# Feed-forward and conv outputs made one tile at a time, from all inner tiles

## The chip, the cores and the metric

The kernel runs on one core of one Trainium2 chip. A time is device microseconds (us) of one execution, the median of several. A core has five engines that run side by side, each in its own order: TensorE (PE in the profile: matrix products, with its weight loads shown apart as PEld), VectorE (DVE), ScalarE (ACT), GpSimd (POOL), and SyncE (SP), which starts most DMAs. On-chip memory is SBUF; PE writes into PSUM, eight banks of 128 x 512 floats here.

## The reference, cut to what matters

A trunk of two layers over 256 tokens of 1024 features, in full fp32. Each layer has a feed-forward, a mixer (attention with pooling in layer 0, a short convolution in layer 1), and another feed-forward; each of these six sub-layers takes a normed input that a vector c shifts and scales, and is added to the stream through a gate that c drives too.

```
mod = (silu(c) @ w_ada[l] + b_ada[l])                       # 9 vectors of 1024 per layer: shift, scale, gate x 3
h = rmsnorm(x, norm_g[l, j]) * (1 + scale) + shift
x = x + 0.5 * gate * ((silu(h @ wg) * (h @ wu)) @ wd)       # feed-forward: 1024 -> 2816 -> 1024
x = x + gate * mixer(h)                                     # attention and pooling, or conv
```

## The kernel before, in words

**Layout.** Features lie on partitions, tokens along the free dimension: a feature tile is 128 x 256. The stream x is eight such tiles, `xt`. A feed-forward has 22 inner tiles (2816 = 22 x 128).

**Products.** A product of 128 x 128 weights with a tile is made of three matmuls of 256 columns: high weights by high activations, low weights by high, high by low (`mm`, L312). "High" is a value rounded to fp32r, "low" what is left. Weights arrive by DMA into `raw` (four slots of 2 MB) and are split on the chip: ACT casts the high part `wh` (L357), then DVE or, every fourth time, POOL subtracts to give the low part `wl` (L373). Five buffers hold split weights, some 8 to 12 us ahead of their use.

**Steps.** The program is a list of steps in the order of PE's work, most of them 24 matmuls: a step has its products, what evacuates them (`post`), and work that is put off by one or two steps. The order on every engine is this program order; each engine runs its own list strictly in that order.

**Feed-forward.** The inner tiles come in six chunks of 3 or 4: gate products, up products, then the chunk's down products, which are added for all eight output tiles in four PSUM banks. The last chunk's down steps (12 matmuls per output tile) finish the output tiles one after the other: DVE adds gate times result to the stream in SBUF (L660), `take` lets ACT make the square and the high part of the next sub-layer's input, and two steps later DVE adds the square to the sum of squares (L498) and makes the low part (L499).

**Norm put off.** The next sub-layer doesn't wait for its norm. Its first seven products (six in attention, eight in conv; `raw_steps`) take x * g * (1 + scale), called `xh` and `xl`, with 258 columns. When the sum of squares is complete, PE sums it over the partitions (`total`, L506), DVE works out 1 / rms, PE spreads it (L523), and DVE copies it to `rtile` (L527). Then POOL (`nx` L531, `nh` L541), ACT (`ah` L542) and DVE (`al` L546) make the eight normed tiles that all later products take. In a feed-forward the seven products are those of the first chunk (3 gates, 3 ups) and one gate of the second; the first chunk's down products come next, and they take only the first chunk's activations.

**Modulation in the background.** The vectors that c drives need 128 more multiply-adds of 128 x 1024 rows on DVE ("macs", `ada_mac`, L160 and L162). Each takes one 512 KB transfer (`adaw`, four buffers). Eight or sixteen macs make one accumulator `acc`; PE then transposes it (L189) and DVE reduces it (L193). `RATES` says how many macs are handed out per step; `flush` hands out at once, in one row, all that the next sub-layer still needs, and the transposes behind them. `flush` is called on entering the last chunk's up steps and down steps, the conv's first output step, and a step of attention.

## Time and profile before

| | |
|---|---|
| time, median of 3 runs | 1089.36 us (1088.84 to 1092.68) |
| span of the profiled execution | 1092.0 us |
| PE busy | 1014.1 us, 93% of the span |
| DVE busy | 824.7 us, 76% |
| ACT busy, POOL busy | 503.7 us, 462.5 us |
| DMA, share of 16 engines | 61.6% |

The profile is of one execution. A busy time is the sum over an engine's instructions; since matmuls overlap, PE's pace is better read from the starts of two matmuls. PE runs at one of two granted clocks, 1.2 or 2.4 GHz; the profile gives the mean as a share of the full one (0.957 over the whole span).

### The profile page before, as it was taken

How to read it: one execution, taken by the hardware profiler on the slowest of the kernel's cores; microseconds unless marked ns; L12 is line 12 of the kernel's file. 1: busy time of each engine (PE TensorE's matmuls, PEld its weight loads, DVE VectorE, ACT ScalarE, POOL GpSimd, SP SyncE). 2: the span in 40 equal slices, each digit the busy share in tenths (PEclk: the TensorE clock that was granted, in tenths of full speed). 3: DMA queues.
4: the chain of work that ended last, by engine and by line, in shares of the span. 5: the costliest groups of instructions: out<-in, count | busy, mean ns of one | idle time of the engine just before them, and what ended most of it. 6: DMA issues, size and time to landing. Idle time of an engine off the chain costs nothing.

```text
span 1092.0 us, 19601 instructions
## 1 busy us (share of the span) xinstructions
PE 1014.1 (93%) x7894; PEld 986.1 (90%) x7894; DVE 824.7 (76%) x1118; ACT 503.7 (46%) x905; POOL 462.5 (42%) x346
## 2 busy tenths in 40 slices
PE   3799999998698799999998999999899989999998
PEld 2799999988567799999997999999889988999998
DVE  3857876888988889799888978896778788534442
ACT  3344544445445554345454544345554455444453
POOL 6712322265943672232166522234664567112223
PEclk9789999998879899999998999999999989999999
DMA  9588998773173429988865497996344534735601
GB/s 349 206 307 297 335 359 311 261 264 125 59 270 111 159 94 361 355 304 319 298 243 188 189 351 265 352 359 231 107 152 155 173 117 147 275 122 209 232 1 40
DMA packets 98634, 247.15 MB, mean 226 GB/s; under 512 B 4768, under 2 KB 22228, under 8 KB 98544
## 3 DMA queue, kind: packets, MB, share of 16 engines
q1 hardware_dynamic: 98288, 245.78, 61.6%
q8 instruction: 62, 1.02, 0.4%
q14 instruction: 28, 0.23, 0.1%
q0 software_dynamic: 256, 0.12, 0.0%
HBM read 244.84 MB, written 1.05 MB: 225 GB/s over the span
## 4 chain that ended last, share of the span: by engine, by line
PE 69%; DVE 17%; issue 6%; POOL 5%; ACT 2%; DMA 0%; SPq 0%; DVEq 0%; ACTq 0%; POOLq 0%
PE pu L312 41%; PE acc L312 25%; DVE acc L162 5%; DVE ssum L498 3%; POOL nh L541 2%; POOL nx L531 2%; DVE wl L373 2%; ACT wh L357 1%; DVE xt L660 1%; DVE xl L499 1%; POOL ssum L1407 1%; DVE al L322 1%; PE pu L1310 1%; PE pu L1015 1%; DVE rs_t L439 0%
## 5 line engine op out<-in xcount | busy, mean ns | idle before, releaser
L373 POOL TENSOR_TENSOR wl<-raw,wh 128x1024 fp32r<-128x1024 f32 (+1 forms) x162 | 328.3, 2038 | 528.8 <-ACT wh L357 443.0
L357 ACT CAST wh<-raw 128x1024 fp32r<-128x1024 f32 (+2 forms) x408 | 345.1, 860 | 136.7 <-PE acc L312 86.8
L312 PE MATMUL pu<-ah,wh 128*128 128x256 f32 x1304 | 371.4, 285 | 0.4 <-ACT ah L542 0.4
L312 PE MATMUL pu<-al,wh 128*128 128x256 f32 x1304 | 370.3, 284 | 0.5 <-DVE al L546 0.5
L312 PE MATMUL pu<-ah,wl 128*128 128x256 f32 x1304 | 370.2, 284 | 0.0
L373 DVE TENSOR_TENSOR wl<-raw,wh 128x1024 fp32r<-128x1024 f32 (+2 forms) x246 | 271.1, 1110 | 74.5 <-ACT wh L357 74.4
L312 PE MATMUL acc<-ah,wh 128*128 128x256 f32 x896 | 259.3, 289 | 10.3 <-ACT ah L319 6.5
L312 PE MATMUL acc<-al,wh 128*128 128x256 f32 x896 | 257.8, 288 | 3.2 <-DVE al L322 3.2
L312 PE MATMUL acc<-ah,wl 128*128 128x256 f32 x896 | 256.8, 287 | 0.0
L312 PEld LDWEIGHTS pu<-al,wh 128*128 128x128 f32 x1304 | 251.3, 193 | 0.9 <-DVE al L546 0.9
L312 PEld LDWEIGHTS pu<-ah,wh 128*128 128x128 f32 x1304 | 251.4, 193 | 0.7 <-ACT ah L542 0.7
L312 PEld LDWEIGHTS pu<-ah,wl 128*128 128x128 f32 x1304 | 251.4, 193 | 0.2 <-POOL wl L373 0.2
L162 DVE SCALAR_TENSOR_TENSOR acc<-adaw,cact,acc 128x1024 f32<-128x1024 f32 x119 | 197.1, 1656 | 0.4
L312 PEld LDWEIGHTS acc<-ah,wh 128*128 128x128 f32 x896 | 176.0, 196 | 11.3 <-ACT ah L319 7.3
L312 PEld LDWEIGHTS acc<-al,wh 128*128 128x128 f32 x896 | 175.4, 196 | 4.4 <-DVE al L322 4.3
L312 PEld LDWEIGHTS acc<-ah,wl 128*128 128x128 f32 x896 | 175.7, 196 | 0.0
L319 ACT CAST ah<-sg 128x256 fp32r<-128x256 f32 x88 | 35.6, 407 | 172.1 <-DVE sg L705 157.2
L705 DVE TENSOR_TENSOR sg<-pu,sg 128x256 f32<-128x256 f32 x75 | 31.5, 420 | 79.8 <-PE pu L312 79.6
L312 PE MATMUL pu<-xl,wh 128*128 128x258 f32 x200 | 65.2, 326 | 23.1 <-DVE xl L499 22.3
L697 ACT ACTIVATE sg<-pu 128x256 f32<-128x256 f32 x72 | 27.4, 383 | 111.1 <-PE pu L312 111.1
L312 PEld LDWEIGHTS pu<-xl,wh 128*128 128x128 f32 x200 | 43.3, 216 | 28.6 <-DVE xl L499 28.6
L531 POOL TENSOR_TENSOR nx<-xt,rtile 128x256 f32<-128x256 f32 x48 | 47.3, 990 | 43.0 <-DVE rtile L527 40.9
(187 smaller groups left out, 1117.7 us busy)
## 6 DMA issues: line engine op xcount, KB each, us to landing
adaw<-in_w_ada_dram SPq DMA_DIRECT2D x128, 512.0 KB, 5.7
raw<-in_ffn_wd_dram SPq DMA_DIRECT2D x16, 2048.0 KB, 9.2
raw<-in_ffn_wu_dram SPq DMA_DIRECT2D x15, 2048.0 KB, 10.6
raw<-in_ffn_wg_dram SPq DMA_DIRECT2D x14, 2048.0 KB, 10.3
raw<-in_ffn_wg_dram SPq DMA_DIRECT2D x8, 1536.0 KB, 7.1
raw<-in_ffn_wu_dram SPq DMA_DIRECT2D x8, 1536.0 KB, 7.2
raw<-in_ffn_wd_dram SPq DMA_DIRECT2D x8, 1536.0 KB, 7.3
raw<-in_w_in_c_dram SPq DMA_DIRECT2D x6, 2048.0 KB, 7.8
```

The costliest lines, as they stand in the source:

```text
L162: nc.vector.scalar_tensor_tensor(out=acc, in0=w, scalar=scales[:, k:k + 1], in1=acc, op0=ALU.mult, op1=ALU.add)
L312: nc.tensor.matmul(ps, lhsT=a[:, k, :], rhs=m, start=start and i == 0, stop=stop and i == n - 1, skip_group_check=True)
L319: nc.scalar.copy(hi, src)
L322: nc.vector.tensor_tensor(out=lo, in0=src, in1=hi.bitcast(F32), op=ALU.subtract)
L357: nc.scalar.copy(shaped(hi, r), r)
L373: eng.tensor_tensor(out=shaped(lo, r), in0=r, in1=shaped(hi, r).bitcast(F32), op=ALU.subtract)
L498: nc.vector.tensor_tensor(out=self.s, in0=self.s, in1=q, op=ALU.add)
L499: nc.vector.scalar_tensor_tensor(out=lo[:, 0:T], in0=xt[d], scalar=g, in1=hi[:, 0:T].bitcast(F32), op0=ALU.mult, op1=ALU.subtract)
L531: nc.gpsimd.tensor_tensor(out=a, in0=xt[t], in1=rtile[:, 0:T], op=ALU.mult)
L541: (eng or nc.gpsimd).tensor_scalar(out=h, in0=a, scalar1=g, scalar2=s, op0=ALU.mult, op1=ALU.add)
L697: nc.scalar.activation(out=s, in_=v, func=AF.Silu)
L705: nc.vector.tensor_tensor(out=s, in0=v, in1=s, op=ALU.mult)
```

## The change

- Down products (and the conv's output products) are made one output tile at a time, from all inner tiles: for each of the eight tiles d three steps of 8, 8 and 6 inner tiles (`DOWN`; one step of 8 in conv). All gate and up products come before them, in the order gate, gate, up, up. The chunks are gone, and with them their own buffers for the last chunk's weights.
- High and low activations stand side by side in one tile, so a down product is two matmuls instead of three (`mm2`): high weights by both, 512 columns, and low weights by the high one, 256 columns. The two halves of the PSUM bank are added when the tile is finished.
- `finish` updates the stream inside PSUM: DVE u = b * gate + xt, DVE a = a * gate + u in PSUM; ACT takes the high part, the copy to `xt` and the square from PSUM, DVE the low part and the sum of squares with one operand in PSUM. Low part one step later, sum two steps later; for the last tile both at once.
- Up products stay in PSUM: they are multiplied by the gate there, and split from there.
- Of the deferred products, the first step now takes seven pieces of the input, the second four, then the first step's eighth; `total` stands behind that, ahead of the rest of the second step.
- Weights are fetched in eight slots of 1 MB (256 columns of gate, up and down weights) instead of four of 2 MB.
- `RATES` of the feed-forwards is 0.6, 0.7 and 0.7 macs per step instead of 1.3, 1.3 and 1.4; it counts the down steps in full, where each was counted 0.6 (the last chunk's not at all). `flush` is entered at the third down step of tile 0.
- The result's transposes are put off by one step instead of two, and its last transfers are cut at tiles 6 and 7.

The diff, cut to its core:

```
-FIRST = (4, 4, 3, 3, 4, 4)
-CHUNKS = (3, 3, 4, 4, 4, 4)
-SLOT = 4096
+NF = DFF // P
+OWN = 14
+DOWN = (8, 8, 6)
+SLOT = 2048
...
-ADAB, RAWB = 4, 4
+ADAB, RAWB = 4, 8
...
-RATES = ((-3, 1.3), (4, 1.9), (0, 1.3), (0, 1.4), (1, 1.1), (1, 1.0))
+RATES = ((-3, 0.6), (4, 1.9), (0, 0.7), (0, 0.7), (1, 1.1), (1, 1.0))
...
+    def mm2(bank_, w, xs, start, stop, ks):
+        wh, wl = w
+        both = bank_.rearrange("p (a t) -> p a t", a=2)
+        for i, k in enumerate(ks):
+            x = xs[k]
+            nc.tensor.matmul(both, lhsT=wh[:, i, :], rhs=x, start=start and i == 0, stop=False, skip_group_check=True)
+            nc.tensor.matmul(bank_[:, 0:T], lhsT=wl[:, i, :], rhs=x[:, 0, :], start=False, stop=stop and i == len(ks) - 1,
+                             skip_group_check=True)
...
-        def take(self, d):
+        def take(self, d, a, b):
             g = self.gsc[:, d:d + 1]
             hi, lo = self.xs[d]
-            q = self.square(d)
-            nc.scalar.activation(out=hi[:, 0:T], in_=xt[d], func=AF.Copy, scale=g)
+            nc.scalar.activation(out=hi[:, 0:T], in_=a, func=AF.Copy, scale=g)

             def rest():
-                if q is not None:
-                    nc.vector.tensor_tensor(out=self.s, in0=self.s, in1=q, op=ALU.add)
-                nc.vector.scalar_tensor_tensor(out=lo[:, 0:T], in0=xt[d], scalar=g,
+                nc.vector.scalar_tensor_tensor(out=lo[:, 0:T], in0=a, scalar=g,
                                                in1=hi[:, 0:T].bitcast(F32), op0=ALU.mult, op1=ALU.subtract)
-            return rest
+                nc.scalar.copy(xt[d], a)
...
+                nc.scalar.activation(out=a if b is None else b, in_=a, func=AF.Square)
+
+            def total():
+                if d:
+                    nc.vector.tensor_tensor(out=self.s, in0=a if b is None else b, in1=self.s, op=ALU.add)
+            return rest, total
...
                     if i == 0:
                         st["w0"] = w
-                        mm(st[0], w, self.xs, True, False, range(6))
+                        mm(st[0], w, self.xs, True, False, range(KT - 1))
                     elif i == 1:
-                        mm(st[1], w, self.xs, True, False, range(6))
-                        mm(st[0], st["w0"], self.xs, False, True, range(6, KT))
-                        mm(st[1], w, self.xs, False, True, range(6, KT))
+                        mm(st[1], w, self.xs, True, False, range(4))
+                        mm(st[0], st["w0"], self.xs, False, True, range(KT - 1, KT))
                         self.total()
+                        mm(st[1], w, self.xs, False, True, range(4, KT))
...
+    def finish(d, a, b, gate, target):
+        g = gate[:, d:d + 1]
+        r = xt[d]
+        if b is not None:
+            u = scr.tile([P, T], F32, name=nm("u"), tag="nh")
+            nc.vector.scalar_tensor_tensor(out=u, in0=b, scalar=g, in1=r, op0=ALU.mult, op1=ALU.add)
+            r = u
+        nc.vector.scalar_tensor_tensor(out=a if isinstance(target, Norm) else xt[d], in0=a, scalar=g, in1=r,
+                                       op0=ALU.mult, op1=ALU.add)
+        if not isinstance(target, Norm):
+            return target.take(d)
+        rest, total = target.take(d, a, b)
+        if d < KT - 1:
+            return [(1, rest), (2, total)]
+        rest()
+        total()
+        return []
...
+    def major_steps(acts, piece, parts, gate, target, width=0, ticks=1.0):
+        box = {}
+        k0 = len(steps)
+        starts = [sum(parts[:i]) for i in range(len(parts))]
+        for d in range(KT):
+            for i, (f0, n) in enumerate(zip(starts, parts)):
+                final = i == len(parts) - 1
...
+                    mm2(box[d], w, xs, i == 0, final and m == n, range(f0, f0 + m))
...
+                add(Step(pe, raw=piece(d, i), post=post, ticks=ticks, cost=3 * n,
+                         keep=int(final and d + 1 < width)))
+        def enter():
+            flush()
+            get_ready(target, [0])
+        steps[k0 + len(parts) - 1].enter = enter
...
-                nc.vector.tensor_tensor(out=s, in0=v, in1=s, op=ALU.mult)
+                nc.vector.tensor_tensor(out=v, in0=v, in1=s, op=ALU.mult)
+                s = v
...
+        for f in range(8 if norm.start else 0, NF, 2):
+            order += [(0, f), (0, f + 1), (1, f), (1, f + 1)]
...
+        for which, f in order:
+            plain(which, f)
+        major_steps(lambda: acts, down_piece, DOWN, lambda: gate_vec(layer, 2 + 6 * j, True), target)
```

**DVE where the down products begin.** Before, in the second feed-forward of layer 0, where the up products of a chunk end and its down products begin: `sg` is gate times up, `al` an activation's low part, `wl` a split of weights, `acc` a mac.

```order
L162 SCALAR_TENSOR_TENSOR acc_5245<-adaw_5319,cact_90,acc_5245 128x1024
L373 TENSOR_TENSOR wl_5531<-raw_5288,wh_5492 128x512
L322 TENSOR_TENSOR al_5524<-sg_5384,ah_5523 128x256
L705 TENSOR_TENSOR sg_5418<-pu_5536,sg_5418 128x256
L162 SCALAR_TENSOR_TENSOR acc_5245<-adaw_5353,cact_90,acc_5245 128x1024
L373 TENSOR_TENSOR wl_5570<-raw_5288,wh_5568 128x512
L322 TENSOR_TENSOR al_5563<-sg_5418,ah_5562 128x256
L162 SCALAR_TENSOR_TENSOR acc_5245<-adaw_5387,cact_90,acc_5245 128x1024
L373 TENSOR_TENSOR wl_5605<-raw_5288,wh_5603 128x512
L162 SCALAR_TENSOR_TENSOR acc_5245<-adaw_5421,cact_90,acc_5245 128x1024
L373 TENSOR_TENSOR wl_5638<-raw_5288,wh_5634 128x512
```

After, where the down products begin (the second row is the low part of the last activation, now in `xp`):

```order
L761 TENSOR_TENSOR pu_5497<-pu_5497,sg_5455 128x256
L332 TENSOR_TENSOR xp_5523<-pu_5497,xp_5523 128x256
L161 SCALAR_TENSOR_TENSOR acc_5347<-adaw_5268,cact_90,acc_5347 128x1024
L380 TENSOR_TENSOR wl_5554<-raw_4961,wh_5525 128x1024
L161 SCALAR_TENSOR_TENSOR acc_5347<-adaw_5349,cact_90,acc_5347 128x1024
L161 SCALAR_TENSOR_TENSOR acc_5347<-adaw_5424,cact_90,acc_5347 128x1024
L161 SCALAR_TENSOR_TENSOR acc_5347<-adaw_5490,cact_90,acc_5347 128x1024
L161 SCALAR_TENSOR_TENSOR acc_5347<-adaw_5550,cact_90,acc_5347 128x1024
L161 SCALAR_TENSOR_TENSOR acc_5347<-adaw_5575,cact_90,acc_5347 128x1024
L161 SCALAR_TENSOR_TENSOR acc_5347<-adaw_5578,cact_90,acc_5347 128x1024
L161 SCALAR_TENSOR_TENSOR acc_5347<-adaw_5581,cact_90,acc_5347 128x1024
L161 SCALAR_TENSOR_TENSOR acc_5347<-adaw_5584,cact_90,acc_5347 128x1024
```

Macs that stood singly among the splits of weights now stand in one run of twelve, behind one more mac and one split; the last four of the run are left out here.

**PE at that place.** Before, the transposes (L189) of that accumulator stand among the products of a chunk's gate step:

```order
L312 MATMUL pu_5854<-ah_4463,wh_5728 128x256
L312 MATMUL pu_5854<-ah_4463,wl_5747 128x256
L312 MATMUL pu_5854<-al_4464,wh_5728 128x256
L189 MATMUL misc_5883<-ident,acc_5245 128x128 x4
L312 MATMUL pu_5894<-ah_4301,wh_5745 128x256
L312 MATMUL pu_5894<-ah_4301,wl_5781 128x256
L312 MATMUL pu_5894<-al_4302,wh_5745 128x256
```

After, they stand between the second and the third down step of tile 0 (`wh_5426` is the second step's, `wh_5457` the third's):

```order
L322 MATMUL acc_5532<-xp_5057,wh_5426 128x512
L323 MATMUL acc_5532<-xp_5057,wl_5459 128x256
L322 MATMUL acc_5532<-xp_5093,wh_5426 128x512
L323 MATMUL acc_5532<-xp_5093,wl_5459 128x256
L188 MATMUL misc_5611<-ident,acc_5347 128x128 x4
L188 MATMUL pu_5616<-ident,acc_5347 128x128 x4
L322 MATMUL acc_5532<-xp_5195,wh_5457 128x512
L323 MATMUL acc_5532<-xp_5195,wl_5494 128x256
```

The transposes take the finished accumulator, and the products of tile 0 stand behind them.

**DVE at the end of a feed-forward.** Before, in the first one, where the last output tiles are finished and the next sub-layer's input is made:

```order
L660 SCALAR_TENSOR_TENSOR xt_108<-acc_775,hg_2644,xt_108 128x256
L498 TENSOR_TENSOR ssum_2647<-ssum_2647,sq_2724 128x256
L499 SCALAR_TENSOR_TENSOR xl_2565<-xt_107,gsc_2466,xh_2564 128x256
L660 SCALAR_TENSOR_TENSOR xt_109<-acc_776,hg_2644,xt_109 128x256
L498 TENSOR_TENSOR ssum_2647<-ssum_2647,sq_2742 128x256
L499 SCALAR_TENSOR_TENSOR xl_2569<-xt_108,gsc_2466,xh_2568 128x256
L660 SCALAR_TENSOR_TENSOR xt_110<-acc_777,hg_2644,xt_110 128x256
L498 TENSOR_TENSOR ssum_2647<-ssum_2647,sq_2762 128x256
L499 SCALAR_TENSOR_TENSOR xl_2610<-xt_109,gsc_2466,xh_2609 128x256
L498 TENSOR_TENSOR ssum_2647<-ssum_2647,sq_2782 128x256
L499 SCALAR_TENSOR_TENSOR xl_2614<-xt_110,gsc_2466,xh_2613 128x256
```

After, the last two tiles:

```order
L161 SCALAR_TENSOR_TENSOR acc_2136<-adaw_2237,cact,acc_2136 128x1024
L636 SCALAR_TENSOR_TENSOR u_2458<-acc_2399,hg_2010,xt_109 128x256
L638 SCALAR_TENSOR_TENSOR acc_2399<-acc_2399,hg_2010,u_2458 128x256
L483 TENSOR_TENSOR xp_2462<-mod_1971,xp_2462 128x2
L502 SCALAR_TENSOR_TENSOR xp_2384<-acc_2399,gsc_1987,xp_2384 128x256
L161 SCALAR_TENSOR_TENSOR acc_2136<-adaw_2289,cact,acc_2136 128x1024
L513 TENSOR_TENSOR ssum_2025<-acc_2399,ssum_2025 128x256
L192 TENSOR_REDUCE modr_2492<-misc_2518 128x4
L636 SCALAR_TENSOR_TENSOR u_2540<-acc_2472,hg_2010,xt_110 128x256
L638 SCALAR_TENSOR_TENSOR acc_2472<-acc_2472,hg_2010,u_2540 128x256
L502 SCALAR_TENSOR_TENSOR xp_2462<-acc_2472,gsc_1987,xp_2462 128x256
L513 TENSOR_TENSOR ssum_2025<-acc_2472,ssum_2025 128x256
```

The low parts and the sums take their input from `acc`, which is in PSUM, instead of from `xt` and `sq` in SBUF, and the rows of one tile are parted from those of the next by splits and macs.

**PE at the end of the deferred products.** Before, in that same second feed-forward, the seventh deferred product (`xl`, `xh`) is followed by the first chunk's down products:

```order
L312 MATMUL pu_4425<-xh_4017,wh_4216 128x258
L312 MATMUL pu_4425<-xh_4017,wl_4315 128x258
L312 MATMUL pu_4425<-xl_4018,wh_4216 128x258
L312 MATMUL acc_4476<-ah_4296,wh_4249 128x256
L312 MATMUL acc_4476<-ah_4296,wl_4317 128x256
L312 MATMUL acc_4476<-al_4297,wh_4249 128x256
```

After, by a gate product that takes the normed tiles:

```order
L311 MATMUL pu_4190<-xp_3783,wh_3988 128x258
L311 MATMUL pu_4190<-xp_3783,wl_4085 128x258
L311 MATMUL pu_4190<-xp_3783,wh_3988 128x258
L311 MATMUL pu_4239<-xp_4073,wh_4021 128x256
L311 MATMUL pu_4239<-xp_4073,wl_4087 128x256
L311 MATMUL pu_4239<-xp_4073,wh_4021 128x256
```

Both rows go on from the deferred products' last matmul; what stands next takes activations before, and normed tiles after.

## Rows read from the trace of the kernel before

**Rows 1.** The page, parts 1 and 4: busy us by engine; the chain of waits by engine.

```profile
PE 1014.1 (93%) x7894; PEld 986.1 (90%) x7894; DVE 824.7 (76%) x1118; ACT 503.7 (46%) x905; POOL 462.5 (42%) x346
...
PE 69%; DVE 17%; issue 6%; POOL 5%; ACT 2%; DMA 0%; SPq 0%; DVEq 0%; ACTq 0%; POOLq 0%
```

**Rows 2.** PE's waits, whole span: us in total, times, longest us.

```profile
PE pu L312 <- DVE xl L499: 22.3, 14, 3.5
...
PE pu L1310 <- DVE acc L162: 5.8, 1, 5.8
...
PE misc L189 <- DVE acc L162: 0.5, 2, 0.2
```

**Rows 3.** Timeline, PE, where the second feed-forward ends: start us, us, instruction.

```profile
574.07 0.28 PE L312 MATMUL pu<-xh,wh 128*128 128x258 f32 x1
...
578.78 0.58 PE L312 MATMUL pu<-xl,wh 128*128 128x258 f32 x1 [3.22 <-DVE xl L499]
...
587.95 0.50 PE L506 MATMUL misc<-ones,ssum 128*128 128x1 f32 x4
```

**Rows 4.** Windows from first deferred product to total: us, busy us by engine, granted clock, DMA.

```profile
365.70:381.30 15.60, 9.90 (x52) 9.07 (x50) 13.20 (x15) 6.84 (x14) 9.30 (x4) 0.67 0.43 152
574.00:588.00 14.00, 9.74 (x52) 8.50 (x51) 12.94 (x14) 5.45 (x11) 9.33 (x4) 0.76 0.53 194
```

**Rows 5.** Timeline, DVE and POOL, of the same stretch.

```profile
576.17 2.56 DVE L499 SCALAR_TENSOR_TENSOR xl<-xt,gsc,xh 128x256 fp32r<-128x256 f32 x1
...
579.04 0.41 DVE L498 TENSOR_TENSOR ssum<-ssum,sq 128x256 f32<-128x256 f32 x1
...
567.91 10.53 POOL L373 TENSOR_TENSOR wl<-raw,wh 128x512 fp32r<-128x512 f32 x5 [6.22 <-ACT wh L357]
```

**Rows 6.** Groups by line, DVE, whole span: busy us, mean ns, idle before.

```profile
L162 DVE SCALAR_TENSOR_TENSOR acc<-adaw,cact,acc 128x1024 f32<-128x1024 f32 x119 | 197.1, 1656 | 0.4
L499 DVE SCALAR_TENSOR_TENSOR xl<-xt,gsc,xh 128x256 fp32r<-128x256 f32 x40 | 53.1, 1327 | 0.0
...
L498 DVE TENSOR_TENSOR ssum<-ssum,sq 128x256 f32<-128x256 f32 x35 | 35.3, 1008 | 1.3 <-ACT sq L486 1.3
...
L660 DVE SCALAR_TENSOR_TENSOR xt<-acc,hg,xt 128x256 f32<-128x256 f32 x32 | 15.0, 478 | 13.9 <-PE acc L312 13.9
```

**Rows 7.** Timeline, PE at full clock: 512 columns, then 256 columns.

```profile
272.01 0.40 PE L903 MATMUL acc<-wh,al 128*128 128x512 f32 x1
...
275.43 0.39 PE L903 MATMUL acc<-wh,al 128*128 128x512 f32 x1
...
435.74 0.28 PE L312 MATMUL pu<-ah,wl 128*128 128x256 f32 x1
...
437.66 0.28 PE L312 MATMUL pu<-al,wh 128*128 128x256 f32 x1
```

**Rows 8.** Timeline, DVE and POOL, norm of the third feed-forward.

```profile
593.36 0.42 DVE L527 COPY rtile<-misc 128x256 f32<-128x256 f32 x1 [0.90 <-PE misc L523]
...
611.58 0.42 DVE L546 TENSOR_TENSOR al<-nh,ah 128x256 fp32r<-128x256 f32 x1 [0.46 <-POOL nh L541]
...
593.87 0.74 POOL L531 TENSOR_TENSOR nx<-xt,rtile 128x256 f32<-128x256 f32 x1 [7.94 <-DVE rtile L527]
...
603.40 0.60 POOL L541 TENSOR_SCALAR nh<-nx,gsc,mod 128x256 f32<-128x256 f32 x1
```

**Rows 9.** PE's waits behind those deferred products (587 to 630).

```profile
PE acc L312 <- ACT ah L319: 2.0, 1, 2.0
```

**Rows 10.** Macs of line 162: duration ns min/median/max, first and last start.

```profile
L162 DVE SCALAR_TENSOR_TENSOR acc<-adaw,cact,acc x119: 1267/1276/3474, 94.3 to 747.0; 128x1024 f32<-128x1024 f32 x119
```

**Rows 11.** Timeline, DVE, macs in a row at the program's start.

```profile
44.20 12.29 DVE L162 SCALAR_TENSOR_TENSOR acc<-raw,cact,acc 128x1024 f32<-128x1024 f32 x7
```

**Rows 12.** DMA issues: KB each, median us to landing.

```profile
adaw<-in_w_ada_dram SPq DMA_DIRECT2D x128, 512.0 KB, 5.7
```

**Rows 13.** Window behind a PE wait of 7.69 us (attention).

```profile
299.00:305.00 6.00, 5.47 (x17) 4.72 (x18) 5.96 (x4) 1.68 (x4) 5.92 (x4) 0.50 0.08 11
```

More of the change, by code (lines that the diff above doesn't have):

```diff
@@ L83, in __init__ @@
         self.cost = (COST if raw is None else 24 * COST_MM) if cost is None else cost * COST_MM
-        self.away, self.keep, self.hold, self.w = None, keep, 0.0, None
+        self.keep, self.hold, self.w = keep, 0.0, None
 @with_exitstack
@@ L338, in shaped @@
         return v.rearrange("p (a b) -> p a b", a=r.shape[1])
-    live = {}
-    def home(s):
-        if s.away is not None and HBUF:
-            return s.away["pool"], "dw", HBUF
-        return unitp, "w", UBUF
+    live = [0]
     def split_high(until):
@@ L659, in evacuate @@
                     for e, r in enumerate(region(box["accs"], d, dn)):
-                        nc.vector.scalar_tensor_tensor(out=xt[d + e], in0=r, scalar=box["gate"][:, d + e:d + e + 1],
-                                                       in1=xt[d + e], op0=ALU.mult, op1=ALU.add)
-                    for e in range(dn):
-                        more = last[1].take(d + e)
-                        late += more if isinstance(more, list) else [(TLATE, more)]
-                for p in prepare:
-                    for e in range(dn):
-                        if (d + e) in p[1]:
-                            p[0].prepare(p[1][d + e])
@@ L669, in evacuate @@
-                return late
-            out_.append(add(Step(pe, raw=Part(load, pick), post=post, lo=lo, ticks=ticks, keep=int(d + dn < width),
-                                  cost=3 * dn * (load.args[1] if nk is None else nk))))
+                        late += finish(d + e, r, None, box["gate"], last[1])
+                if prepare is not None:
+                    get_ready(prepare, range(d, d + dn))
+                return late
+            raw, n = picks(d)
+            out_.append(add(Step(pe, raw=raw, post=post, lo=lo, ticks=ticks, cost=3 * dn * n)))
@@ L694, in gate_out, with piece @@
-        def gate_out(ci, f, v, bias=None):
-            s = box["pool"].tile([P, T], F32, name=nm("sg"), tag=f"sg{f}")
+            for which, f0 in ((0, 0), (1, 0), (0, 4)):
+                halves[which, f0] = [Load((wg, wu)[which][4 * h * P:4 * (h + 1) * P, f0 * P:(f0 + 4) * P], 4, 4 * P)
+                                     for h in range(2)]
+            lead_loads.extend(halves[k][h] for h in range(2) for k in ((0, 0), (1, 0), (0, 4)))
+        loads = {}
+        def piece(which, f):
+            k = which, f // 2
+            if k not in loads:
+                c0 = (f - f % 2) * P
+                loads[k] = Load((wg, wu)[which][:, c0:c0 + 2 * P], KT, 2 * P)
+            return Part(loads[k], lambda v: v[:, :, (f % 2) * P:(f % 2 + 1) * P])
@@ L696, in gate_out, with down_piece @@
+        def down_piece(d, i):
+            k = 2, d // 2, i
+            if k not in loads:
+                f0, c0 = sum(DOWN[:i]), (d - d % 2) * P
+                loads[k] = Load(wd[f0 * P:(f0 + DOWN[i]) * P, c0:c0 + 2 * P], DOWN[i], 2 * P)
+            return Part(loads[k], lambda v: v[:, :, (d % 2) * P:(d % 2 + 1) * P])
+        def gate_out(f, v, bias=None):
+            s = box["pool"].tile([P, T], F32, name=nm("sg"), tag="sg", bufs=4)
             if bias is None:
@@ L1125, in pick @@
             def pick(v):
[L1126 removed]
+                return v[:, 4 * u:4 * u + 4, :]
             def pe(w):
@@ L1198, in part @@
             return [Part(ld, lambda v, f=f: v[:, :, f * P:(f + 1) * P]) for f in range(m)]
-        rc, rb, rx = [part(o, 4) + part(o + 4, 4) for o in (KT, 0, 2 * KT)]
+        rc, rb, rx = [sum((part(o + f, 2) for f in range(0, KT, 2)), []) for o in (KT, 0, 2 * KT)]
         def c_out(t, v, b=None):
```

261 lines of the change are left out of this document (109 added, 152 removed).

## The prediction

> **What bounds the kernel now.** I read the engines first: PE is busy 93% of the span and holds 69% of the chain of waits, DVE 17% [rows 1]. So a change gains by giving PE less to do or by taking its waits away, and loses by making PE wait. Next PE's waits: the largest is for `xl`, 22.3 us in 14 pieces [rows 2], and all of it lies where a sub-layer ends and the next one's deferred products begin. There I took windows. At the end of the second feed-forward PE does 48 matmuls of 258 columns between the first deferred product at 574.07 and `total` at 587.95 [rows 3]. At the full-clock pace of 0.12 us [rows 7] they need 5.8 us; they took 13.9, with a wait of 3.22 us [rows 3] and a mean granted clock of 0.76 [rows 4]. Behind attention it is 15.6 us at 0.67 [rows 4]. The five such places (the other three 13.4, 13.9 and 13.8 us, the same pattern) take 70.7 us instead of 29: 41.7 us lost.
>
> Why DVE is late there shows in its timeline. Eight output tiles are finished within 12 us, and the operations on two SBUF inputs stretch while POOL makes its splits: 2.56 us for a low part that takes about 0.5 alone, during POOL's 10.53 us of splits [rows 5]. Over the span L499 means 1327 ns and L498 1008 ns, while L660, one input in PSUM, means 478 ns [rows 6].
>
> **Products.** The change makes two matmuls of 512 and 256 columns from three of 256. At full clock 16 matmuls of 256 columns lie between 435.74 and 437.66, 120 ns each, and 15 of 512 between 272.01 and 275.43, 228 ns each [rows 7]. A product goes from 360 to 348 ns. There are 4 x 22 x 8 + 8 x 8 = 768: -9.2 us, all on PE's path. The ends are 0 and -10. A Trainium skill rule speaks against this term: "TensorE: Matmul & The Clock Gate", section "Back-to-back issue gap", puts the isolated gap at columns / 2.4 GHz plus 2.5 ns, so one matmul fewer would save 2.5 ns; the term would then be an estimated -1.9 us and the sum 7.3 us higher. The rows here show 13 to 14 ns above the columns' time, so the sum goes by the rows.
>
> **Ends of sub-layers.** One output tile is now finished per 22 products, 7.7 us of PE, and its DVE work is four operations with a PSUM input, at some 0.48 us each [rows 6]. Only the last tile's is left at the border: u, a, ACT's high part, the low part, about 2 us with handovers. PE covers it by 33 matmuls, 7 pieces of the first step and 4 of the second, 4.0 us. I keep 0.5 us for each of three feed-forward ends, 1 behind conv and 3.5 behind attention, where two tiles a step still finish, in 12 matmuls, 1.44 us of PE, against six operations, 2.7 us, of DVE: 6 of the 41.7 us. That is -35, between -28 and -41.
>
> **Normed tiles.** What covered their making is gone. Before, the first chunk's down products lay behind the seven deferred ones, and PE waited there 2.0 us for an activation [rows 9], at each of three feed-forwards. Now a gate product follows that takes all eight normed tiles. From `rtile` at 593.36 to the last `al` at 612.0 it took 18.6 us [rows 8], POOL's two operations and one split setting the pace. `rtile` stands behind 84 deferred matmuls, so it comes about 11 us after the first of them; the last normed tile then at about 29.5. PE is through its 168 deferred matmuls at 20.2 and wants the last tile 2.5 us later: it waits some 6 to 7 us, in pieces, with about 1 us of half clock. Against 2.0 before that is +4.7 for each of three: +14. If POOL's pair runs at 0.74 + 0.60 us [rows 8] throughout, the tiles are ready 5 us sooner and the term is 0; the upper end is 20.
>
> **The macs.** Fewer macs per step are handed out in the feed-forwards, so the rest is handed out at once when `flush` comes at tile 0's third down step. DVE's row has a run of 10 there in the first feed-forward, 12 in the second and 5 in the third, each behind one more mac and a split; the transposes stand on PE ahead of the third down step's products. PE, in order, has nothing else: it does the first two down steps, 16 products, 5.6 us, and then waits for the last mac. Before, PE lost 0.5 us in two waits to such macs [rows 2], as they were spread. A mac takes 1.27 us alone (the median is 1.276), 1.66 in the mean [rows 6, 10]. DVE starts its run about 1.6 us after the last up product (product, high, low part). Second feed-forward: 13 macs and a split end at 1.6 + 13 x 1.28 + 1.3 = 19.5, so PE waits 14 us; at 1.66 it waits 19. First: 11 macs and a split, 12 to 15.6, with one stop while the accumulator's buffer is turned over. Third: 5 to 7. That is 31 to 42 us; I take 36, since only four rows are in place ahead and the next must be fetched, 5.7 us each [rows 12], four at a time. Behind such a wait the clock is half: after PE's 7.69 us wait in attention the window of 6 us shows 0.50 [rows 13], 1.2 GHz, which costs nearly 3 us, three times 2.7. Together +44, between 34 and 52. A wait of this kind is in the trace already: at the start seven macs in a row take DVE 12.29 us [rows 11], and PE waits 5.8 us for them [rows 2].
>
> **Small terms.** Up products stay longer in their three PSUM banks; product, high and low part take about 3 us and two more steps, 5.8 us, pass before the bank is wanted: +1, at worst 8. Weight runs of 1 KB instead of 2 KB: DMA is not what PE waits for anywhere after the start; nothing, covered by eight slots filled ahead; were that cover gone, it is rival four's. Waits of the last chunk's down products for late activations go: -2. Start and tail stay within 1.
>
> **Sum.** -9.2 - 35 + 14 + 44 + 1 - 2 = +12.8 on a profiled 1092.0, so about 1105. The profiled span lies 2.6 us above the median, so the time is 1102.
>
> **Rivals.** (1) *The macs don't hold PE.* If DVE is through its run when PE gets to the transposes, the 44 falls away and the sum is -31: 1058. It decides at 31 us: below that the change is no longer slower. For it: DVE has slack, 24% of the span. Against: the run stands behind the last activation's low part, which itself waits for PE. (2) *Normed tiles in time, macs at their low end.* 0 instead of 14, 34 instead of 44: -11, 1078. For it: fewer macs stand beside POOL then. Against: the splits of weights stay beside it. (3) *The gains are smaller*: two matmuls pace like three, and PE still waits at the borders for half of what it lost: +12.8 + 9 + 16 = +38, 1127. For it: DVE's splits now lie between the tiles' rows. (4) *Banks or 1 KB runs bind*: up to +10 on the sum, 1112. For it: DMA is at 0.53 of its engines even in the window of a border [rows 4].
>
> **How the numbers follow.** Forecast 1102, chance 0.52, its own range 1090 to 1112. Rival 1: 0.13; rival 2: 0.15; rival 3: 0.10; rival 4: 0.10. 0.5% of 1089, 5.4 us, is about what a measurement of this kernel can tell from no change. Rival 1 and most of rival 2 give faster: 0.25. The forecast's lower edge, the rest of rival 2, gives same: 0.15. Slower keeps 0.60. The range leaves out rival 1 and the far part of rival 3: 1074 to 1120.
>
> **What would show it.** In the changed kernel's profile: PE's waits at the transposes of `acc` of 12 to 16, 14 to 19 and 5 to 7 us, each with half clock behind it. The waits for the low part `xp` at the borders under 2 us at feed-forward ends. Waits of PE for `nh` or `al` of about 6 us in each of three feed-forwards. A pitch of 348 ns for a pair in the down steps. The forecast is wrong if the transposes wait under 31 us in all, or if the borders still lose 15.

## The result, and the profile after

The changed kernel takes 1149.74 us (1149.36 to 1149.99), the kernel before 1090.51 us beside it: a ratio of 1.0535, 95% interval 1.0514 to 1.0556. It is slower, as forecast, but by 59 us instead of 12, and outside the range. The profiled execution has a span of 1148.0 us, 56 more than before. One of the ten executions of e8_three below took 1581.74 us at a granted clock of 0.56; it counts in the median given there, not in the ratio.

The page of the changed kernel, its span, engines and chain of waits:

```profile
span 1148.0 us, 18170 instructions
...
PE 1010.1 (88%) x7126; PEld 941.4 (82%) x7126; DVE 783.1 (68%) x1134; ACT 500.7 (44%) x873; POOL 418.1 (36%) x298
...
PE 66%; DVE 19%; issue 4%; POOL 4%; DMA 4%; ACT 3%; SPq 0%; DVEq 0%; ACTq 0%; POOLq 0%
```

Against [rows 1] PE is busy 4 us less, and every other engine is busy less too: no engine got more work. The 56 us are to be looked for in PE's waits and in its clock, whose mean went from 0.957 to 0.928. PE's waits of the changed kernel (us in total, times, longest) say where:

```profile
PE misc L188 <- DVE acc L161: 40.3, 5, 19.4
PE misc L188 <- DVE modr L192: 14.2, 1, 14.2
...
PE pu L311 <- ACT xp L555: 8.9, 7, 1.8
PE pu L1301 <- DVE xt L638: 8.8, 8, 1.1
PE pu L311 <- DVE xp L502: 7.9, 6, 3.2
...
PE pu L311 <- DVE xp L559: 6.0, 16, 0.6
```

L188 are the transposes of the modulation's accumulators: 54.5 us, where the kernel before waited 1.7 at the same transposes, 0.5 of it for macs [rows 2]. L1301 are the result's transposes, 8.8 us. L502 is the deferred products' low part, the 22.3 us of [rows 2]. L555 and L559 are the normed tiles' high and low parts.

Cut at the first deferred product of each sub-layer (its start in PE's timeline, us from the span's start), the two traces compare so:

| from, to | before | after | more |
|---|---|---|---|
| start, attention's first (245.82; 256.83) | 245.8 | 256.8 | +11.0 |
| to the second feed-forward's (365.73; 380.99) | 119.9 | 124.2 | +4.3 |
| to the third's (574.07; 615.23) | 208.3 | 234.2 | +25.9 |
| to conv's (780.53; 826.45) | 206.5 | 211.2 | +4.7 |
| to the last feed-forward's (883.59; 930.13) | 103.1 | 103.7 | +0.6 |
| to the end (1092.0; 1148.0) | 208.4 | 217.9 | +9.5 |

The largest single wait stands in the second feed-forward. PE's timeline of the changed kernel has the four long waits for macs, and one of the tail's eight (start, us, instruction, idle before and what ended it):

```profile
196.58 1.08 PE L188 MATMUL misc<-ident,acc 128*128 128x128 f32 x4 [14.18 <-DVE modr L192]
...
365.31 1.09 PE L188 MATMUL misc<-ident,acc 128*128 128x128 f32 x4 [9.46 <-DVE acc L161]
...
556.39 1.12 PE L188 MATMUL misc<-ident,acc 128*128 128x128 f32 x4 [19.41 <-DVE acc L161]
...
767.31 1.11 PE L188 MATMUL misc<-ident,acc 128*128 128x128 f32 x4 [8.41 <-DVE acc L161]
...
1088.67 0.44 PE L1301 MATMUL pu<-ident,xt 128*128 128x128 f32 x2 [1.10 <-DVE xt L638]
```

DVE's timeline ahead of the one at 556.39, where the run of macs forced by `flush` is:

```profile
535.43 3.91 DVE L161 SCALAR_TENSOR_TENSOR acc<-adaw,cact,acc 128x1024 f32<-128x1024 f32 x3
539.88 1.29 DVE L161 SCALAR_TENSOR_TENSOR acc<-adaw,cact,acc 128x1024 f32<-128x1024 f32 x1 [0.53 <-DMA adaw<-in_w_ada_dram]
543.83 5.25 DVE L161 SCALAR_TENSOR_TENSOR acc<-adaw,cact,acc 128x1024 f32<-128x1024 f32 x4 [2.67 <-DMA adaw<-in_w_ada_dram]
549.24 1.28 DVE L161 SCALAR_TENSOR_TENSOR acc<-adaw,cact,acc 128x1024 f32<-128x1024 f32 x1 [0.17 <-DMA adaw<-in_w_ada_dram]
551.39 1.28 DVE L161 SCALAR_TENSOR_TENSOR acc<-adaw,cact,acc 128x1024 f32<-128x1024 f32 x1 [0.86 <-DMA adaw<-in_w_ada_dram]
553.70 2.64 DVE L161 SCALAR_TENSOR_TENSOR acc<-adaw,cact,acc 128x1024 f32<-128x1024 f32 x2 [1.02 <-DMA adaw<-in_w_ada_dram]
```

Every mac of this run takes 1.3 us, the price of a mac alone in [rows 10], and from the fourth on DVE also waits for the transfers, 5.3 us in all (a piece with x3 or x4 is that many in a row). The window over that run shows the DMA engines at 0.95, POOL idle, PE idle until the transposes in the last 1.6 us, and a mean clock of 0.55. Its numbers are start:end and length in us, then the busy us of PE, PEld, DVE, ACT and POOL with the number of instructions, the granted clock, the DMA share and GB/s:

```profile
537.00:558.00 21.00, 1.61 (x8) 1.61 (x9) 14.33 (x12) 0.00 (x0) 0.00 (x0) 0.55 0.95 344
```

### The profile page after: what moved, and what is told of

It reads as the page before. It is cut to its first block, busy times and chain, and to the rows that moved or that the text cites. A ratio compares the mean times of both kernels' runs of the same rounds, so it can differ in the third digit from the quotient of the medians.

```text
span 1148.0 us, 18170 instructions
## 1 busy us (share of the span) xinstructions
PE 1010.1 (88%) x7126; PEld 941.4 (82%) x7126; DVE 783.1 (68%) x1134; ACT 500.7 (44%) x873; POOL 418.1 (36%) x298
## 4 chain that ended last, share of the span: by engine, by line
PE 66%; DVE 19%; issue 4%; POOL 4%; DMA 4%; ACT 3%; SPq 0%; DVEq 0%; ACTq 0%; POOLq 0%
PE pu L311 38%; PE acc L322 14%; PE acc L323 7%; DVE acc L161 6%; DVE wl L380 3%; DMA adaw<-in_w_ada_dram 3%; PE acc L311 2%; POOL nx L544 2%; ACT wh L365 1%; DVE a L332 1%; POOL nh L554 1%; POOL ssum L1433 1%; DVE tx L573 1%; DVE xp L559 1%; PE pu L1336 1%
## 5 line engine op out<-in xcount | busy, mean ns | idle before, releaser
L311 PE MATMUL pu<-xp,wh 128*128 128x256 f32 (+1 forms) x3008 | 562.9, 288 | 24.2 <-ACT xp L555 8.9
L380 POOL TENSOR_TENSOR wl<-raw,wh 128x1024 fp32r<-128x1024 f32 (+2 forms) x114 | 287.2, 2527 | 626.0 <-ACT wh L365 451.9
L311 PEld LDWEIGHTS pu<-xp,wh 128*128 128x128 f32 x3008 | 476.2, 193 | 33.4 <-ACT xp L555 11.4
L311 PE MATMUL pu<-xp,wl 128*128 128x256 f32 (+1 forms) x1504 | 429.4, 285 | 1.5 <-DVE wl L380 0.9
L365 ACT CAST wh<-raw 128x1024 fp32r<-128x1024 f32 (+1 forms) x336 | 336.0, 1006 | 83.2 <-PE acc L322 35.5
L380 DVE TENSOR_TENSOR wl<-raw,wh 128x1024 fp32r<-128x1024 f32 (+1 forms) x222 | 276.9, 1258 | 43.8 <-ACT wh L365 43.8
L311 PEld LDWEIGHTS pu<-xp,wl 128*128 128x128 f32 x1504 | 292.2, 194 | 2.2 <-DVE wl L380 1.3
L161 DVE SCALAR_TENSOR_TENSOR acc<-adaw,cact,acc 128x1024 f32<-128x1024 f32 x119 | 180.2, 1514 | 12.9 <-DMA adaw<-in_w_ada_dram 12.2
L322 PE MATMUL acc<-a,wh 128*128 128x512 f32 x512 | 183.6, 401 | 2.1 <-DVE a L332 2.1
L323 PE MATMUL acc<-a,wl 128*128 128x256 f32 x512 | 144.3, 282 | 0.0
L311 PEld LDWEIGHTS acc<-xp,wh 128*128 128x128 f32 x416 | 68.1, 197 | 3.4 <-ACT xp L555 3.2
L311 PE MATMUL acc<-xp,wl 128*128 128x256 f32 (+1 forms) x208 | 59.9, 288 | 0.2 <-POOL wl L380 0.2
L322 PEld LDWEIGHTS acc<-xp,wh 128*128 128x128 f32 x256 | 49.8, 195 | 12.0
```

The source lines that it names most:

```text
L161: nc.vector.scalar_tensor_tensor(out=acc, in0=w, scalar=scales[:, k:k + 1], in1=acc, op0=ALU.mult, op1=ALU.add)
L311: nc.tensor.matmul(ps, lhsT=a[:, k, :], rhs=m, start=start and i == 0, stop=stop and i == n - 1, skip_group_check=True)
L322: nc.tensor.matmul(both, lhsT=wh[:, i, :], rhs=x, start=start and i == 0, stop=False, skip_group_check=True)
L323: nc.tensor.matmul(bank_[:, 0:T], lhsT=wl[:, i, :], rhs=x[:, 0, :], start=False, stop=stop and i == len(ks) - 1, skip_group_check=True)
L365: nc.scalar.copy(shaped(hi, r), r)
L380: eng.tensor_tensor(out=shaped(lo, r), in0=r, in1=shaped(hi, r).bitcast(F32), op=ALU.subtract)
```

## The experiments

The theory was: the forced macs cost nearly all, the tail's eight waits the next, and the rest is gains that came out smaller. The rivals are in each expectation. "The kernel before" is run beside each group, with medians between 1090.5 and 1093.5 us, so ratios (with their 95% intervals) are compared across groups. A ratio can differ by 0.001 from the quotient of the two medians.

**e1_rates: the macs handed out as before.**

```
-RATES = ((-3, 0.6), (4, 1.9), (0, 0.7), (0, 0.7), (1, 1.1), (1, 1.0))
+RATES = ((-3, 1.3), (4, 1.9), (0, 1.3), (0, 1.4), (1, 1.1), (1, 1.0))
```

> The changed kernel with the macs handed out as before (1.3, 1.3 and 1.4 per step in the feed-forwards). Theory, the macs forced at tile 0's third down step hold PE: the transposes of acc then wait under 3 us in all instead of 54.5 us (15.3, 9.5, 19.4, 8.4 and 1.9), and with the half clock behind each the time falls by 55 to 70 us, to 1080 to 1095. Rival, macs spread over the gate and up steps stretch the splits of weights there and PE waits for wl instead: the transposes' waits go, but the time falls by 30 us or less, to 1120 or more.

Measured: 1108.78 us, 1.0154 (1.0126 to 1.0181) of the kernel before. The direction holds and the size doesn't: 41 us fell away, not 55 to 70. The waits at the transposes fell from 54.5 to 14.7 us, and the time by about as much; 11.5 us of what is left stands in attention, where the transposes now stand ahead of those of q and k. PE's timeline of e1_rates:

```profile
298.78 1.09 PE L188 MATMUL misc<-ident,acc 128*128 128x128 f32 x4 [11.46 <-DVE acc L161]
...
300.65 1.11 PE L1018 MATMUL misc<-ident,qn 128*128 128x128 f32 x4 [0.78 <-DVE modr L192]
```

In the kernel before, PE waits 7.7 us at this place for q and k themselves, so some 4 us of it are new.

**e2_turn2: the result's transposes two steps late again.**

```
-            return [(1, turn)]
+            return [(2, turn)]
```

> The changed kernel with the result's transposes put off by two steps again instead of one. Theory, eight waits of 1.1 us in the last feed-forward are for the tile's two DVE operations and would be covered by one more step: -8 us, to about 1141. Rival, the tail then grows by what was saved: the same time, 1148 to 1151.

Measured: 1140.28 us, 1.0444 (1.0422 to 1.0467): 9.5 us less than the changed kernel. Of the eight waits of 1.1 us one is left. The theory holds.

**e3_three: three matmuls per product again.**

```
-            nc.tensor.matmul(both, lhsT=wh[:, i, :], rhs=x, ...)
+            nc.tensor.matmul(bank_[:, 0:T], lhsT=wh[:, i, :], rhs=x[:, 0, :], ...)
+            nc.tensor.matmul(bank_[:, T:2 * T], lhsT=wh[:, i, :], rhs=x[:, 1, :], ...)
             nc.tensor.matmul(bank_[:, 0:T], lhsT=wl[:, i, :], rhs=x[:, 0, :], ...)
```

> The changed kernel with three matmuls of 256 columns per down and conv output product instead of 512 and 256. Theory from the rows (348 against 360 ns a product): 768 x 12 ns = +9 us, to about 1159. Rival, the Trainium skill's isolated gap of 2.5 ns per matmul: +2 us, about 1152.

Measured: 1148.96 us, 1.0523 (1.0496 to 1.0550), against 1.0535 (1.0514 to 1.0556) with two. No gain from two matmuls shows. Since long waits lie among these products, that was repeated without them, in e8 and e12.

**e4_before_rates: the kernel before with the changed rates alone.** The edit of e1_rates the other way round, on the kernel before.

> The kernel before with only the changed rates of the macs (0.6, 0.7 and 0.7 per step in the feed-forwards). Theory, it is the forced macs that cost and not the new order of products: runs of 4, 11, 5, 4 and 7 macs stand ahead of transposes on DVE, PE waits at them for 25 to 40 us in all, and the time rises by 25 to 50 us, to 1115 to 1140. Rival, the chunked order hides them behind other products: under 1100.

Measured: 1160.50 us, 1.0633 (1.0605 to 1.0662): 68 us slower than the kernel before, slower even than the changed kernel. Scarce macs alone, in the old order of products, cost more than the whole change. More than expected, too: PE's waits of e4_before_rates have 59.9 us at the transposes.

```profile
PE misc L189 <- DVE acc L162: 59.9, 5, 22.5
```

**e5_even: one mac per step, attention's later, and the tail of e2.**

```
-RATES = ((-3, 0.6), (4, 1.9), (0, 0.7), (0, 0.7), (1, 1.1), (1, 1.0))
+RATES = ((-3, 1.0), (-3, 1.9), (0, 1.0), (0, 1.0), (1, 1.1), (1, 1.0))
...
-            return [(1, turn)]
+            return [(2, turn)]
```

> The changed kernel with one mac per step in every feed-forward, attention's macs begun a little later (so that their transposes stand behind the q and k transposes), and the result's transposes put off by two steps. Theory, the extra time is forced macs and the tail and nothing else of size: no wait at the transposes of acc above 3 us, and 1108.8 less 8.5 for the tail and 8 for the 11.5 us wait in attention: 1090 to 1096. Rival, the macs' transfers fill the DMA engines beside the 1 KB weight runs (they are at 1.0 in the gate and up steps of the kernel with the old rates) and waits for wl and adaw stay: 1100 or more.

Measured: 1092.55 us, 1.0002 (0.9988 to 1.0017), as expected: with the two causes taken away the slowdown is gone, 47.7 us for the macs (against e2_turn2) and 9.5 for the tail. `tick` never lets more than one mac gather (`BURST`), so 1.0 and 1.3 both mean one per step, and anything from 0.5 to under 1 means one in two steps: that is why 0.6 or 0.7 lets half of them pile up. But the forecast's other terms should have left a gain of 31 us, and none is left. From first deferred product to `total` the five borders take 46.9 us in e5_even (9.8, 16.9, 7.4, 4.3, 8.4) against 37.7 in the changed kernel (4.4, 16.9, 4.3, 4.3, 7.7), so spread macs take 9.2 us back there. One such place shows in e5_even's timelines at the end of the second feed-forward, of DVE and then of POOL:

```profile
581.15 3.04 DVE L161 SCALAR_TENSOR_TENSOR acc<-adaw,cact,acc 128x1024 f32<-128x1024 f32 x1
...
584.45 3.07 DVE L161 SCALAR_TENSOR_TENSOR acc<-adaw,cact,acc 128x1024 f32<-128x1024 f32 x1
587.44 0.47 DVE L636 SCALAR_TENSOR_TENSOR u<-acc,hg,xt 128x256 f32<-128x256 f32 x1
```

```profile
580.48 14.91 POOL L380 TENSOR_TENSOR wl<-raw,wh 128x1024 fp32r<-128x1024 f32 x5 [1.23 <-ACT wh L365]
```

Macs now stand in the last tiles' steps; beside POOL's splits (five in 14.91 us) they take 3 us, and the last tile's `u` stands behind them.

**e6_att: the end of attention in SBUF.** In `finish`, for attention's tiles alone (no `b`):

```
-        nc.vector.scalar_tensor_tensor(out=a if isinstance(target, Norm) else xt[d], in0=a, scalar=g, in1=r,
+        nc.vector.scalar_tensor_tensor(out=a if isinstance(target, Norm) and b is not None else xt[d], in0=a, scalar=g, in1=r,
```

and `take` reads `xt[d]` there instead of `a`, with no copy.

> The kernel of e5_even with the stream updated in SBUF again at the end of attention (only the square goes to PSUM). Theory, 12.5 us are lost there because DVE and ACT take turns on the one PSUM bank that two tiles share (4.1 us per pair of tiles): with the stream in SBUF the turns go, and the stretch from first deferred product to total falls from 16.9 to 10 us or less, the time by 5 to 9 us. Rival, the SBUF operations stretch beside POOL as in the kernel before (15.6 us there): within 2 us of e5_even.

Measured: 1090.07 us, 0.9990 (0.9972 to 1.0007), 2.5 us less than e5_even by the medians, 0.0012 by the ratios, which is within the intervals. From first deferred product to `total` it takes 14.0 us instead of 16.9: between the theory and the rival.

**e7_raw8: eight deferred products in a feed-forward, on e6_att.**

```
-RAW_UNITS = 7
+RAW_UNITS = 8
```

> The kernel of e6_att with eight deferred products in each feed-forward instead of seven, as conv has. Theory, PE waits 4.4 to 4.9 us in each of three feed-forwards for normed tiles, plus half clock, since nothing covers their making: one more deferred product covers 2.9 us, so 3 to 4.5 us less each, -9 to -13 us. Rival, the eighth product's bank and DVE work delay the tiles by as much: within 3 us of e6_att.

Measured: 1078.42 us, 0.9872 (0.9820 to 0.9924): 11.7 us less than e6_att, as the theory has it. The size is uncertain: the four executions took 1073.5, 1083.4, 1073.5 and 1083.4 us, and the interval of the ratio allows 7 to 19 us. The direction is clear of it. The trace is of one of the two shorter ones; its span is 15.1 us below that of e6_att's trace. PE's waits for the normed tiles, first of e6_att, then of e7_raw8:

```profile
PE pu L311 <- ACT xp L557: 8.7, 7, 1.8
...
PE pu L311 <- DVE xp L561: 6.5, 16, 0.6
```

```profile
PE pu L311 <- ACT xp L557: 6.2, 4, 2.0
...
PE pu L311 <- DVE xp L561: 3.5, 7, 0.6
```

The waits fall by 5.5 us. Most of the rest goes with the clock. Windows of 20 us over the first gate products of the three feed-forwards show it, of e6_att and then of e7_raw8 (the granted clock is the third number from the end):

```profile
395.00:415.00 20.00, 15.64 (x91) 13.62 (x91) 16.51 (x20) 10.36 (x16) 11.14 (x11) 0.74 0.50 165
604.00:624.00 20.00, 15.07 (x95) 13.12 (x94) 16.79 (x20) 10.61 (x17) 11.42 (x11) 0.83 0.48 149
904.00:924.00 20.00, 14.97 (x92) 13.03 (x91) 12.19 (x17) 10.37 (x16) 11.09 (x11) 0.83 0.47 142
```

```profile
394.30:414.30 20.00, 16.97 (x128) 16.36 (x127) 18.99 (x23) 9.99 (x16) 11.24 (x10) 0.91 0.66 215
596.50:616.50 20.00, 17.22 (x115) 16.31 (x114) 18.67 (x22) 10.09 (x16) 10.84 (x10) 0.83 0.66 213
896.30:916.30 20.00, 16.98 (x139) 16.37 (x138) 15.81 (x21) 11.75 (x19) 10.18 (x8) 1.00 0.59 180
```

The share missing to 1.00, times 20 us, is 12.0 us in the first and 5.2 in the second, 6.8 less. With fewer and shorter waits PE stays at 2.4 GHz more of the time.

**e8_three: three matmuls per product, on e6_att.** The edit of e3_three.

> The kernel of e6_att with three matmuls of 256 columns per down and conv output product. With the forced macs gone the pace of PE sets the time: 768 products at 10 ns more, +7 to +9 us. By the Trainium skill's 2.5 ns per matmul +2 us. Rival, PE's pace in the down steps is not what sets the time: within 2 us.

Measured: 1090.29 us, 0.9986 (0.9972 to 1.0001), against 0.9990 with two: the rival. The pace did change. PE's timelines in the last feed-forward, where PE doesn't wait: of e6_att, 13 products from one row to the other, 4.54 us, 349 ns each;

```profile
1029.79 0.40 PE L322 MATMUL acc<-a,wh 128*128 128x512 f32 x1
...
1034.33 0.40 PE L322 MATMUL acc<-a,wh 128*128 128x512 f32 x1
```

of e8_three, 15 products from one to the other, 5.36 us, 357 ns each:

```profile
1029.28 0.28 PE L321 MATMUL acc<-xp,wh 128*128 128x256 f32 x1
...
1034.64 0.28 PE L321 MATMUL acc<-a,wh 128*128 128x256 f32 x1
```

Over all products that follow each other at full clock (some 730 of the 768, those with 300 to 400 ns from start to start) the means are 352 and 358 ns. So two matmuls save 6 ns, not 12, some 5 us over 768 products, and the border behind conv gives 2.6 us of it back (8.4 us there from first deferred product to `total`, 5.8 with three). Of DVE's rows at that border one differs by more than 0.1 us, the last tile's shift column: 2.35 us in e6_att, 0.16 in e8_three. The last section takes it up.

**e9_banks: attention's end in PSUM, two tiles of a step in two banks, otherwise as e7_raw8.**

```
-        return [accs[e // 2][:, (e % 2) * T:(e % 2 + 1) * T] for e in range(d, d + dn)]
+        return [accs[e % 4][:, (e // 4) * T:(e // 4 + 1) * T] for e in range(d, d + dn)]
```

> As e7_raw8, but with the end of attention done in PSUM as in the changed kernel, and the two tiles of a step in two different banks. Theory of the bank taken in turns: the stretch from attention's last step to total is then no longer than e7_raw8's 14.0 us, nearer 10, and the time 1073 to 1079. Rival, the turns are between the two engines and not about the bank: 16.9 us as in the changed kernel, and 1080 to 1083.

Measured: 1075.03 us, 0.9840 (0.9816 to 0.9864), and 7.1 us from first deferred product to `total` instead of 16.9. The macs are spread here and scarce in the changed kernel, but that changes nothing at this place: with spread macs and one bank (e5_even) it is 16.9 us too. In the changed kernel DVE and ACT took turns there, each waiting for the other's operation (its timelines of DVE, then of ACT):

```profile
384.96 0.48 DVE L638 SCALAR_TENSOR_TENSOR acc<-acc,mod,xt 128x256 f32<-128x256 f32 x1
386.14 0.49 DVE L638 SCALAR_TENSOR_TENSOR acc<-acc,mod,xt 128x256 f32<-128x256 f32 x1 [0.70 <-ACT xp L499]
```

```profile
385.65 0.46 ACT L499 ACTIVATE xp<-acc,gsc 128x256 fp32r<-128x256 f32 x1
386.67 0.47 ACT L499 ACTIVATE xp<-acc,gsc 128x256 fp32r<-128x256 f32 x1 [0.56 <-DVE acc L638]
```

With two banks the two tiles' operations follow at once; DVE's timeline of e9_banks:

```profile
361.17 0.87 DVE L638 SCALAR_TENSOR_TENSOR acc<-acc,mod,xt 128x256 f32<-128x256 f32 x2
```

The theory of the bank holds. In the time the 3 us against e7_raw8 are within the intervals of the two, so no gain in the time is shown.

**e10_quiet: no macs in a feed-forward's last two output tiles, on e7_raw8.**

```
-                add(Step(pe, raw=piece(d, i), post=post, ticks=ticks, cost=3 * n,
+                add(Step(pe, raw=piece(d, i), post=post, ticks=ticks if d < 6 else 0, cost=3 * n,
```

> As e7_raw8, but with no macs handed out in the last two output tiles of a feed-forward. Theory, macs spread over all steps take back part of the border's gain (first deferred product to total 9.8 and 7.4 us behind the first and second feed-forward, 4.4 and 4.3 where macs were scarce): both fall below 6 us, 3 to 8 us less in all. Rival, POOL's splits for the first deferred products set those stretches: the same time within 3 us.

Measured: 1068.82 us, 0.9779 (0.9755 to 0.9804): 9.6 us less than e7_raw8's median, 4.7 less than the two shorter of its executions; the direction holds. The two stretches fall from 9.8 and 7.4 us to 4.3 each, 8.5 in all, while the one behind attention is 2.2 us longer in this trace (16.1 against 14.0). The windows from first deferred product to `total` behind the first feed-forward, of e7_raw8 and then of e10_quiet:

```profile
241.70:251.50 9.80, 6.83 (x39) 6.02 (x37) 8.39 (x8) 4.59 (x9) 9.80 (x4) 0.83 1.02 372
```

```profile
243.20:247.50 4.30, 4.30 (x38) 4.30 (x37) 1.88 (x4) 2.08 (x4) 4.30 (x3) 1.00 1.03 363
```

POOL splits throughout both, so its splits alone don't set this stretch; DVE with the macs beside them does, busy 8.4 of 9.8 us with macs and 1.9 of 4.3 without.

**e11_quiet_banks: both edits.**

> Both edits of e9_banks and e10_quiet on e7_raw8. If they are independent, their two differences to e7_raw8 add up.

Measured: 1064.92 us, 0.9742 (0.9723 to 0.9761). The differences in ratio to e7_raw8 are 0.0032 and 0.0093, together 0.0125; measured 0.0130. They add up, as far as e7_raw8's interval (0.0052 either way) lets one say.

**e12_three: e11_quiet_banks with three matmuls per product.**

> The kernel of e11_quiet_banks with three matmuls of 256 columns per down and conv output product. In e8_three's trace such a product takes 354 ns and in e6_att's the pair takes 349 ns in the last feed-forward: 768 x 5 ns = +4 us, to 1068 to 1070. By the prediction's 12 ns +9 us, 1074. Rival, as between e6_att and e8_three: no difference.

Measured: 1062.68 us, 0.9727 (0.9710 to 0.9745), against 0.9742 (0.9723 to 0.9761) with two. No difference a third time, and the shortest time of this study: 2.7% less than the kernel before, and 7.7% less than the changed kernel (0.9727 / 1.0535 = 0.923). The expectation's 354 ns were low for three matmuls; the mean is 358 in e8_three and here.

## Why the prediction was right on the sign and wrong on the size

The sum was +12.8 on the profiled execution; +56 came. By its own terms:

| term | forecast | measured |
|---|---|---|
| products | -9.2 | -5 at PE's pace, 0 in the time |
| ends of sub-layers | -35 | -26 |
| normed tiles | +14 | +7 of waits, and up to 13 of half clock |
| macs | +44 | +53 of waits (54.5 against 1.7) and about 8 of half clock |
| small terms | -1 | not measured by themselves |
| start and tail | within 1 | +9 |

The terms as measured add up to between 46 and 64, and the 56 lie inside.

**Macs: the mechanism was right, its size too small.** The three forecast waits came where they were forecast: 15.3 us in the first feed-forward (1.1 and 14.2; forecast 12 to 15.6), 19.4 in the second (14 to 19), 8.4 in the third (5 to 7). That is 43.1 against 36 taken and 42 at most. Two steps failed. One is the pace, 7 us: the runs also wait for their transfers, which the forecast had named but put in by half; DVE waits 12.2 us for `adaw`, in ten places, all of them in these three runs. The other is the places, 11 us: the macs that were scarce in the first feed-forward's down steps were then missing in attention, 9.5 us, and in conv, 1.9, where the forecast didn't look, since DVE's row shows no long run there. The half clock came as forecast, in four places instead of three. The windows behind the four long waits show

```profile
196.58:202.58 6.00, 6.00 (x25) 5.40 (x26) 4.02 (x12) 1.14 (x2) 0.00 (x0) 0.61 0.54 202
365.30:371.30 6.00, 5.99 (x39) 6.00 (x40) 3.28 (x11) 1.60 (x6) 0.00 (x0) 0.73 0.77 243
556.39:560.00 3.61, 3.61 (x15) 3.37 (x16) 2.22 (x7) 0.67 (x2) 0.00 (x0) 0.55 0.86 259
767.30:771.30 4.00, 3.99 (x15) 3.70 (x16) 2.64 (x8) 0.00 (x0) 0.00 (x0) 0.50 0.71 252
```

so the time missing to full clock is 2.3, 1.6, 1.6 and 2.0 us, about 8. e5_even gives the macs' worth in the time, 47.7 us, net of the 9.2 us that spread macs take at the borders; the two together, 57, are near the 61 read from the trace.

**Ends of sub-layers.** Behind feed-forwards the forecast held, and better: 36 matmuls in 4.3 to 4.4 us, nothing lost, where [rows 4] shows 14.0 for 48. Behind attention it failed: 16.9 us, 12.5 lost instead of the forecast 3.5, because "two tiles a step still finish" was costed as DVE's time alone and not as turns between DVE and ACT on one bank (e9_banks). Behind conv 3.4 are lost instead of 1; 2.2 of them are the last tile's shift column, 2.37 us instead of 0.16 (last section). Lost in all 15.9 instead of 6 of the 41.7, so the forecast's own sign of being wrong, borders that still lose 15, came true.

**Tail.** "Start and tail stay within 1" is the step with the least working behind it. One step less of delay puts each tile's transposes right behind its last product on PE, which then waits for the tile's two DVE operations, 0.48 us each, eight times: 8.8 us (e2_turn2).

**Normed tiles.** The mechanism was right, and the split of the term wrong. The forecast took waits of 6 to 7 us and about 1 us of half clock. PE waits 4.4, 4.3 and 4.9 us there, against 2.3 before (the 2.0 of [rows 9] and 0.26 for `al`), but the clock lost more. Over 32.1 us from `total` on it is 0.82, 0.84 and 0.84 in the three feed-forwards, against 0.95, 0.95 and 1.00 before. The first pair of these windows, before and after:

```profile
381.30:413.40 32.10, 29.79 (x235) 29.38 (x235) 28.24 (x46) 18.93 (x29) 22.40 (x19) 0.95 0.36 127
```

```profile
397.90:430.00 32.10, 27.66 (x182) 25.61 (x182) 25.51 (x46) 16.83 (x25) 18.79 (x19) 0.82 0.32 101
```

That is 16 us missing to full clock against 3, of which the part that falls on PE's waits costs nothing more. So the term lies between 7 and 20; one more product gave back 11.7 us, or 7 to 19 by the interval (e7_raw8).

**Products.** The price of 360 ns from [rows 7] was read from sixteen matmuls; over the span three took 358 in the mean, and two 352 instead of 348. So 6 ns are saved per product instead of 12, and in the time no difference shows in three comparisons. (The rows stand 13 to 15 ns above the columns' time, not 13 to 14.) The Trainium skill's rule that was set against this term ("TensorE: Matmul & The Clock Gate", section "Back-to-back issue gap", 2.5 ns a matmul) is below the 6 ns of pace that the traces show; its estimated 1.9 us can't be told from nothing in the time.

The range failed because macs, ends and tail all ran beyond the ends that the forecast had given them, and products came out at theirs, all on the same side. Rival 3 at 1127 had the small gains, without macs beyond their end. No rival had the tail.

Left open in part: how the 5 us that two matmuls save are lost in full. In all three pairs the border behind conv is shorter with three matmuls: 5.7 against 7.7 us (e3_three, the changed kernel), 5.8 against 8.4 (e8_three, e6_att) and 5.8 against 8.4 (e12_three, e11_quiet_banks). All five borders together are 2.4, 3.4 and 4.8 us shorter. What becomes of the rest is not shown.

## What to carry to other kernels

Work that a scheduler hands out "in the background" has a deadline; halving its rate doesn't save it, it moved it here into one run in front of that deadline, where nothing covered it. Count what is left at the deadline, and find out on which engine's in-order row it stands ahead of other work. When a restructuring takes away the work that stood behind a long chain (here the first chunk's down products), give the chain other cover in the same edit; with the macs spread and kept off the feed-forwards' ends, the result's transposes two steps late, one more deferred product and two banks, the same restructuring is 2.6% faster (e11_quiet_banks) instead of 5.4% slower.
